# A two-layer hybrid decoder step: row sums on VectorE and the late states placed two to a step

## The chip, the cores and the metric

The kernel runs on one core of a Trainium2 chip. The number to be predicted is the device time of one execution in microseconds (us). In the text PE is TensorE, PEld its weight load, DVE is VectorE, ACT ScalarE, POOL GpSimd and SP SyncE.

## The reference

One inference step of a trunk with two layers, for a prompt of 512 tokens and 8 decode sequences of one token, 520 columns in all, in f32. Layer 0 mixes by a gated delta rule, layer 1 by a Mamba-2 scan; each layer goes on with a gated convolutional FFN, and each of the four residual sums is normalised:

```python
x = _layer_norm(DN_ALPHA * x + h, ln1_g[i], ln1_b[i])
f, fb = _conv_ffn(x, ffn_conv[i], ffn_w_up[i], ffn_conv_w[i], ffn_conv_b[i], ffn_w_down[i])
x = _layer_norm(DN_ALPHA * x + f, ln2_g[i], ln2_b[i])

def _conv_ffn(x, buf, w_up, conv_w, conv_b, w_down):
    gv = x @ w_up
    gate, val = gv[..., :D_FF], gv[..., D_FF:]
    gate, new_buf = _causal_dwconv(gate, buf, conv_w, conv_b)
    return (jax.nn.silu(gate) * val) @ w_down, new_buf
```

D_MODEL is 1024, D_FF 2816. Besides the rows, the step returns the new recurrent states of the 8 decode sequences. For layer 1 such a state is `h = exp(dt a) h + dt x B^T` for 32 heads of 64 x 128; these states are not needed by anything that follows in the step.

## The kernel before

Activations lie feature-major: 128 features by 520 columns, two halves h = 0 and 1 of 260. Products in f32 are made of three matmuls with f32r parts (high x high, low x high, high x low). A weight chunk (up to 8 blocks of 128 x 128, `prep`, L214) is loaded into one of two "raw" buffers by ScalarE's queue, its high part "hi" is cast by ScalarE (L229) and its low part "lo" subtracted by VectorE (L230), with three buffers of each; chunks are made two units ahead of TensorE. `unit` (L234) runs one output block: 24 matmuls a half in the up projection, 66 in the down projection, and then the evacuation of that half.

The plan is a list of units. Up projection: nine gate blocks for half 0, five for half 1, then steps m = 0 to 21 that each take gate block m + 4 (one half up to block 8, both from block 9 on) and value block m. A gate block's second half is convolved on VectorE (L423), and the evacuation of a value block makes f = s * psl on VectorE (L482, three buffers f), its high part fh on ScalarE and its low part fl on GpSimd (L285). Down projection: five blocks ("rows" 0 to 4) with both halves, then three blocks for half 0 and three for half 1, which is the tail. A scheduler orders the instructions of every engine before the run, and each engine keeps that order.

The last LayerNorm runs beside the down projection. `ln_evac` makes a row R (L335, or L332 and L312 in the tail) and adds it into the row sum lnacc (L341, L343, L345). After five rows "mean" is made on TensorE from lnacc, ScalarE copies it to lnshift (L347), and rows are shifted by it (L350) and squared (L367), the squares summed on GpSimd (L369). After the eighth row of a half `ln_half` makes "mean" and "var", and then rstd (L382 to L387), subtracts the mean (L390 on GpSimd, L392 on VectorE), multiplies by rstd (L397), scales (L399, L401) and stores o_y.

A late state is one half of the 8 sequences for one pair of heads of layer 1: 32 of them wait in the list `later`. `state` (L994) loads the old state Sd (256 KB) and a row Sr broadcast to 128 partitions (256 KB) by SyncE's queue, multiplies both (L1004, L1005), adds them (L1006), all on GpSimd, and stores o_sdec. A tiny copy of one column into each tile (L999, L1002) holds the load back until its step. `late` takes one state for each of the gate blocks m = 5 to 21 in the up projection, with two buffers of each tile, and three for each of rows 0 to 4 of the down projection, with one buffer. Layer 0 does the same with 16 states, all of which fit beside its up projection.

## Time and profile before

| what | us |
|---|---|
| runs shown | 1798.01, 1792.56, 1792.79 |
| median | 1792.79 |
| the profiled execution | 1798.44 |
| its span | 1796.6 |
| TensorE busy in the span | 1617.7 (90%) |
| VectorE busy | 1202.9 (67%) |
| ScalarE busy | 840.3 (47%) |
| GpSimd busy | 964.4 (54%) |

Busy shares are means over stages of different kind. The change lies in the last quarter: the second up projection ends at 1605.6 us of the span, where the second down projection begins. The first down projection begins at 717 us. Line numbers in the rows are those of the kernel before.

### The profile page before, as it was taken

Reading aid. Unit: us, or ns where it says so; the run is one execution under the profiler, and the core shown is the slowest. Engines: PE = TensorE matmul, PEld = TensorE weight load, DVE = VectorE, ACT = ScalarE, POOL = GpSimd, SP = SyncE. Lnnn points to the kernel's source line nnn. Section 1 sums busy time; section 2 is a strip of 40 time slices with the busy share of each in tenths; the row PEclk is TensorE's granted clock in tenths of the full one; section 3 lists DMA queues with packets and bytes.
Section 4 is the critical chain, followed back from the end, with each engine's and each line's share of the span. In section 5 each row is a group of like instructions: output and inputs, shape, how many; then the busy total and the mean of one; then the engine's idle time right before and its main releaser. Section 6 shows DMA issues by size and latency. Waiting matters only on the chain.

```text
span 1796.6 us, 33707 instructions
## 1 busy us (share of the span) xinstructions
PE 1617.7 (90%) x12889; PEld 1558.6 (87%) x12889; DVE 1202.9 (67%) x2133; ACT 840.3 (47%) x1724; POOL 964.4 (54%) x1090
## 2 busy tenths in 40 slices
PE   8888989898899999999978898989979999999683
PEld 7878888888799999998877797979978999999683
DVE  5967887767776554346799989876486774533255
ACT  4644664344564443125657455535246544432133
POOL 4844777554346554143355757575053565644656
PEclk9999998999999999999999899989999999999897
DMA  5422343234465443335554534332654655435454
GB/s 181 135 84 60 103 136 103 85 113 159 129 201 183 159 165 117 87 96 159 172 147 138 154 120 138 124 103 89 192 169 145 197 179 168 158 121 162 144 159 138
DMA packets 108978, 250.35 MB, mean 139 GB/s; under 512 B 15345, under 2 KB 31697, under 8 KB 108785
## 3 DMA queue, kind: packets, MB, share of 16 engines
q1 hardware_dynamic: 84048, 160.90, 28.3%
q10 hardware_dynamic: 24768, 87.30, 15.7%
q8 instruction: 101, 1.65, 0.4%
q14 instruction: 61, 0.49, 0.1%
HBM read 225.80 MB, written 22.92 MB: 138 GB/s over the span
## 4 chain that ended last, share of the span: by engine, by line
PE 44%; DVE 28%; DMA 13%; ACT 5%; POOL 5%; issue 4%; SPq 1%; ACTq 0%; DVEq 0%; POOLq 0%
PE psl L252 39%; DVE lo L230 4%; DVE sE L1198 3%; DVE y L423 2%; DMA raw<-w_down 2%; DMA Sd<-sstate 2%; ACT hi L229 2%; DMA raw<-w_up 1%; DVE Xtmp L828 1%; DVE kq L423 1%; DMA o_sdec<-Sd 1%; DVE sE L1202 1%; DVE dy L1256 1%; DMA gbc<-gd 1%; POOL Sd L1006 1%
## 5 line engine op out<-in xcount | busy, mean ns | idle before, releaser
L252 PE MATMUL psl<-XH,hi 128*128 128x260 f32 (+1 forms) x2816 | 816.2, 291 | 27.1 <-ACT u L603 8.7
L252 PE MATMUL psl<-XL,hi 128*128 128x260 f32 (+1 forms) x2848 | 822.9, 289 | 7.6 <-DVE XL L409 4.7
L252 PE MATMUL psl<-XH,lo 128*128 128x260 f32 (+1 forms) x2816 | 811.3, 289 | 6.6 <-DVE lo L230 6.2
L252 PEld LDWEIGHTS psl<-XH,hi 128*128 128x128 f32 (+1 forms) x2816 | 540.2, 192 | 36.8 <-ACT u L603 10.2
L230 DVE TENSOR_TENSOR lo<-raw,hi 128x512 fp32r<-128x512 f32 (+2 forms) x439 | 354.3, 842 | 304.6 <-ACT hi L229 300.2
L252 PEld LDWEIGHTS psl<-XL,hi 128*128 128x128 f32 (+1 forms) x2848 | 545.4, 192 | 13.9 <-DVE XL L409 6.2
L252 PEld LDWEIGHTS psl<-XH,lo 128*128 128x128 f32 (+1 forms) x2816 | 539.8, 192 | 13.7 <-DVE lo L230 9.5
L229 ACT CAST hi<-raw 128x512 fp32r<-128x512 f32 (+2 forms) x499 | 314.2, 669 | 401.5 <-PE psl L252 254.2
L252 PE MATMUL psl<-fh,lo 128*128 128x260 f32 x704 | 203.8, 290 | 3.5 <-DVE lo L230 3.4
L252 PE MATMUL psl<-fh,hi 128*128 128x260 f32 x704 | 203.5, 289 | 3.8 <-ACT hi L229 3.8
L252 PE MATMUL psl<-fl,hi 128*128 128x260 f32 x704 | 201.7, 287 | 0.0
L230 POOL TENSOR_TENSOR lo<-raw,hi 128x1024 fp32r<-128x1024 f32 x60 | 148.0, 2467 | 52.0 <-ACT hi L229 50.6
L252 PEld LDWEIGHTS psl<-fh,lo 128*128 128x128 f32 x704 | 135.5, 192 | 5.6 <-DVE lo L230 5.4
L252 PEld LDWEIGHTS psl<-fh,hi 128*128 128x128 f32 x704 | 135.6, 193 | 5.0 <-ACT hi L229 4.5
L252 PEld LDWEIGHTS psl<-fl,hi 128*128 128x128 f32 x704 | 135.3, 192 | 0.3
L285 POOL TENSOR_TENSOR fl<-f,fh 128x260 fp32r<-128x260 f32 x88 | 83.1, 944 | 38.2 <-ACT fh L284 38.2
L423 DVE SCALAR_TENSOR_TENSOR s<-u,par,s 128x512 f32<-128x512 f32 x88 | 77.9, 885 | 6.2 <-ACT s L420 4.4
L482 DVE TENSOR_TENSOR f<-s,psl 128x260 f32<-128x260 f32 x88 | 36.9, 420 | 60.6 <-PE psl L252 59.2
L1005 POOL TENSOR_TENSOR Sd<-Sd,ddt 128x512 f32<-128x512 f32 x32 | 37.0, 1156 | 73.4 <-DMA Sd<-sstate 73.4
L252 PE MATMUL psl<-y,hi 128*128 128x260 f32 x256 | 73.0, 287 | 1.0 <-POOL y L285 0.7
L284 ACT CAST fh<-f 128x260 fp32r<-128x260 f32 x88 | 35.8, 407 | 80.4 <-DVE f L482 80.4
L1006 POOL TENSOR_TENSOR Sd<-Sd,Sr 128x512 f32<-128x512 f32 x48 | 66.2, 1380 | 0.9
(399 smaller groups left out, 2676.2 us busy)
## 6 DMA issues: line engine op xcount, KB each, us to landing
raw<-w_up ACTq DMA_DIRECT2D x106, 512.0 KB
raw<-w_down ACTq DMA_DIRECT2D x44, 512.0 KB
raw<-w_sin SPq DMA_DIRECT2D x43, 512.0 KB
raw<-w_gin SPq DMA_DIRECT2D x32, 512.0 KB
Sd<-sstate SPq DMA_DIRECT2D x64, 256.0 KB
raw<-w_down ACTq DMA_DIRECT2D x22, 384.0 KB
Sd<-gstate SPq DMA_DIRECT2D x32, 256.0 KB
kb<-kr SPq DMA_DIRECT2D x32, 256.0 KB
```

The lines of the kernel that those rows point to most:

```text
L229: nc.scalar.copy(out=hi[:, ks, :mw], in_=raw[:, ks, :])
L230: eng.tensor_tensor(out=lo[:, ks, :mw], in0=raw[:, ks, :], in1=hi[:, ks, :mw].bitcast(F32), op=ALU.subtract)
L252: self.nc.tensor.matmul(out=ps[h][:mw], lhsT=w[:, b0 + k, :mw], rhs=x[:, hs], start=(k0 + k == first and i == 0), stop=(k0 + k == last and ...
L284: nc.scalar.copy(out=hi, in_=xf)
L285: (eng or nc.gpsimd).tensor_tensor(out=lo, in0=xf, in1=hi.bitcast(F32), op=ALU.subtract)
L423: nc.vector.scalar_tensor_tensor(out=y[:, :S], in0=u[:, j:j + S], scalar=self.pcol(wname, i * w + j), in1=y[:, :S], op0=ALU.mult, op1=ALU.add)
L482: nc.vector.tensor_tensor(out=f, in0=ss[m][:, hs], in1=ps, op=ALU.mult)
L828: nc.vector.tensor_tensor(out=tmp[:, :, :, i:], in0=_bc(X16[:, None, :, i:], [P, 2, C, n]), in1=D[:, i:i + 2, :, i:], op=ALU.mult)
L1005: nc.gpsimd.tensor_tensor(out=St, in0=St, in1=_bc(decay[:, :, None], D4), op=ALU.mult)
L1006: nc.gpsimd.tensor_tensor(out=St, in0=St, in1=t, op=ALU.add)
L1198: nc.vector.tensor_scalar(out=E[:, c, :], in0=E[:, c, :], scalar1=self.acum[:, c, h:h + 1], scalar2=0.0, op0=ALU.subtract, op1=ALU.min)
L1202: eng.tensor_tensor(out=E, in0=E, in1=CB, op=ALU.mult)
```

## The change

The row sums of the last LayerNorm (`lni == 3`) go to VectorE. `late` takes a count in place of a number of buffers: in the up projection two states at a gate block while more than 22 are left, else one, and two at each of rows 0 to 4 of the down projection. The tiles Sd and Sr have two buffers in both places. So 22 states lie beside the up projection (two at each of m = 5 to 9, one at each of m = 10 to 21), ten beside the down projection; before it was 17 and 15. Layer 0, with 16 states, keeps one at a gate block.

```diff
+        eng = nc.vector if self.lni == 3 else nc.gpsimd
         if n in (2, NS + 2):
-            nc.gpsimd.tensor_tensor(out=acc, in0=self.R[:, rows[-2], hs], in1=r, op=ALU.add)
+            eng.tensor_tensor(out=acc, in0=self.R[:, rows[-2], hs], in1=r, op=ALU.add)
         elif n not in (1, NS, NS + 1, KD):
-            nc.gpsimd.tensor_tensor(out=acc, in0=acc, in1=r, op=ALU.add)
+            eng.tensor_tensor(out=acc, in0=acc, in1=r, op=ALU.add)
         if n == NS:
-            nc.gpsimd.tensor_tensor(out=acc, in0=acc, in1=r, op=ALU.add)
+            eng.tensor_tensor(out=acc, in0=acc, in1=r, op=ALU.add)
...
-                                self.late(p, u[:, T:T + 1], 2)
+                                self.late(p, u[:, T:T + 1], 2 if len(self.later) > 22 else 1)
...
-                        self.late(lp, self.R[:, m, :1], 1)
+                        self.late(lp, self.R[:, m, :1], 2)
...
-    def late(self, p, after, bufs):
-
-        for _ in range(1 if bufs == 2 else 3):
+    def late(self, p, after, n):
+
+        for _ in range(n):
             if self.later:
                 f, *x = self.later.pop(0)
-                f(p, after, bufs, *x)
+                f(p, after, *x)
...
-        St = p.tile(D4, F32, tag="Sd", name="Sd", bufs=bufs)
+        St = p.tile(D4, F32, tag="Sd", name="Sd", bufs=2)
...
-        t = p.tile(D4, F32, tag="Sr", name="Sr", bufs=bufs)
+        t = p.tile(D4, F32, tag="Sr", name="Sr", bufs=2)
```

The scheduler's order of the two kernels is the same up to the second up projection on every engine. From there it differs on GpSimd and SyncE, from the second down row on VectorE, and from the fifth on ScalarE and TensorE. Lines of the changed kernel after L339 are one higher than those of before.

GpSimd in the second up projection, one step with its state, before:

```order
L999 COPY Sd_16555<-u_16544 128x1
L1002 COPY Sr_16558<-u_16544 128x1
L1005 TENSOR_TENSOR Sd_16555<-Sd_16555,ddt_10608 128x512
L285 TENSOR_TENSOR fl_15776<-f_16599,fh_15775 128x260
L451 MEMSET u_17195 128x2
L1004 TENSOR_TENSOR Sr_16558<-Sr_16558,xdd_10609 128x512
L285 TENSOR_TENSOR fl_15776<-f_16627,fh_15775 128x260
L1006 TENSOR_TENSOR Sd_16555<-Sd_16555,Sr_16558 128x512
L475 COPY cout_15781<-u_16664 128x10
```

The first step with two states, now, from the second state's copies on:

```order
L1000 COPY Sd_16445<-u_16424 128x1
L1003 COPY Sr_16448<-u_16424 128x1
L1006 TENSOR_TENSOR Sd_16435<-Sd_16435,ddt_10608 128x512
L1005 TENSOR_TENSOR Sr_16438<-Sr_16438,xdd_10609 128x512
L285 TENSOR_TENSOR fl_15776<-f_16489,fh_15775 128x260
L452 MEMSET u_17100 128x2
L1006 TENSOR_TENSOR Sd_16445<-Sd_16445,ddt_10608 128x512
L1007 TENSOR_TENSOR Sd_16435<-Sd_16435,Sr_16438 128x512
L1005 TENSOR_TENSOR Sr_16448<-Sr_16448,xdd_10609 128x512
L285 TENSOR_TENSOR fl_15776<-f_16517,fh_15775 128x260
L1007 TENSOR_TENSOR Sd_16445<-Sd_16445,Sr_16448 128x512
L476 COPY cout_15781<-u_16554 128x10
```

A step's two fl and the clearing of the next u stand between the parts of two states instead of one.

GpSimd about the fifth row of the second down projection, before (lnacc at L345 is the row sum that "mean" reads):

```order
L1005 TENSOR_TENSOR Sd_19574<-Sd_19574,ddt_10608 128x512
L1006 TENSOR_TENSOR Sd_19574<-Sd_19574,Sr_19577 128x512
L1002 COPY Sr_19587<-R_19026 128x1
L999 COPY Sd_19584<-R_19026 128x1
L345 TENSOR_TENSOR lnacc_19027<-lnacc_19027,R_19026 128x260
L312 TENSOR_TENSOR xr_20476<-XH_86,XL_87 128x260
L1004 TENSOR_TENSOR Sr_19587<-Sr_19587,xdd_10609 128x512
L345 TENSOR_TENSOR lnacc_19027<-lnacc_19027,R_19026 128x260
L312 TENSOR_TENSOR xr_20574<-XH_86,XL_87 128x260
L1005 TENSOR_TENSOR Sd_19584<-Sd_19584,ddt_10608 128x512
L350 TENSOR_TENSOR R_19026<-R_19026,lnshift_19028 128x260 x3
L1006 TENSOR_TENSOR Sd_19584<-Sd_19584,Sr_19587 128x512
```

The same place now, from the end of the state pair of row 3:

```order
L1007 TENSOR_TENSOR Sd_19790<-Sd_19790,Sr_19793 128x512
L312 TENSOR_TENSOR xr_20476<-XH_86,XL_87 128x260
L312 TENSOR_TENSOR xr_20574<-XH_86,XL_87 128x260
L351 TENSOR_TENSOR R_19076<-R_19076,lnshift_19078 128x260 x3
L370 TENSOR_TENSOR lnsq_19079<-lnsq_19079,sq_19972 128x260
L1000 COPY Sd_19987<-R_19076 128x1
L1003 COPY Sr_19990<-R_19076 128x1
L1000 COPY Sd_19997<-R_19076 128x1
L1003 COPY Sr_20000<-R_19076 128x1
L370 TENSOR_TENSOR lnsq_19079<-lnsq_19079,sq_19976 128x260
L351 TENSOR_TENSOR R_19076<-R_19076,lnshift_19078 128x260 x3
L370 TENSOR_TENSOR lnsq_19079<-lnsq_19079,sq_19980 128x260
```

The row sums are gone from here, and the shift by the mean stands ahead of the last pair of states. VectorE at the same place, before:

```order
L230 TENSOR_TENSOR lo_19929<-raw_19926,hi_19928 128x512 x2
L335 SCALAR_TENSOR_TENSOR R_19026<-xr_19952,psl_19812 128x260
L335 SCALAR_TENSOR_TENSOR R_19026<-xr_20025,psl_19813 128x260
L230 TENSOR_TENSOR lo_20054<-raw_20051,hi_20053 128x512
L230 TENSOR_TENSOR lo_20054<-raw_20051,hi_20053 128x256
L350 TENSOR_TENSOR R_19026<-R_19026,lnshift_19028 128x260
L332 SCALAR_TENSOR_TENSOR xr_20141<-xr_20141,lnshift_19028 128x260
```

And now:

```order
L230 TENSOR_TENSOR lo_19939<-raw_19936,hi_19938 128x512 x2
L335 SCALAR_TENSOR_TENSOR R_19076<-xr_19962,psl_19822 128x260
L346 TENSOR_TENSOR lnacc_19077<-lnacc_19077,R_19076 128x260
L335 SCALAR_TENSOR_TENSOR R_19076<-xr_20025,psl_19823 128x260
L346 TENSOR_TENSOR lnacc_19077<-lnacc_19077,R_19076 128x260
L230 TENSOR_TENSOR lo_20054<-raw_20051,hi_20053 128x512
L230 TENSOR_TENSOR lo_20054<-raw_20051,hi_20053 128x256
L351 TENSOR_TENSOR R_19076<-R_19076,lnshift_19078 128x260 x2
```

Each row sum stands right behind the row that it takes in. On TensorE the first "mean" stands behind 671 of the 1056 down matmuls, before behind 674; in the first down projection it stands behind 674 in both.

GpSimd's last instructions, before:

```order
L1002 COPY Sr_19990<-R_19026 128x1
L999 COPY Sd_19987<-R_19026 128x1
L1004 TENSOR_TENSOR Sr_19990<-Sr_19990,xdd_10609 128x512
L1005 TENSOR_TENSOR Sd_19987<-Sd_19987,ddt_10608 128x512
L1006 TENSOR_TENSOR Sd_19987<-Sd_19987,Sr_19990 128x512
L1002 COPY Sr_20000<-R_19026 128x1
L999 COPY Sd_19997<-R_19026 128x1
L390 TENSOR_TENSOR R_19026<-R_19026,pc_20352 128x260
L1004 TENSOR_TENSOR Sr_20000<-Sr_20000,xdd_10609 128x512
L1005 TENSOR_TENSOR Sd_19997<-Sd_19997,ddt_10608 128x512
L390 TENSOR_TENSOR R_19026<-R_19026,pc_20671 128x260 x5
L1006 TENSOR_TENSOR Sd_19997<-Sd_19997,Sr_20000 128x512
```

And now:

```order
L1007 TENSOR_TENSOR Sd_19987<-Sd_19987,Sr_19990 128x512
L370 TENSOR_TENSOR lnsq_19079<-lnsq_19079,sq_20039 128x260
L1007 TENSOR_TENSOR Sd_19997<-Sd_19997,Sr_20000 128x512
L370 TENSOR_TENSOR lnsq_19079<-lnsq_19079,sq_20043 128x260
L370 TENSOR_TENSOR lnsq_19079<-lnsq_19079,sq_20047 128x260
L370 TENSOR_TENSOR lnsq_19079<-lnsq_19079,sq_20145 128x260
L370 TENSOR_TENSOR lnsq_19079<-lnsq_19079,sq_20244 128x260
L391 TENSOR_TENSOR R_19076<-R_19076,pc_20352 128x260 x5
L370 TENSOR_TENSOR lnsq_19079<-lnsq_19079,sq_20480 128x260
L370 TENSOR_TENSOR lnsq_19079<-lnsq_19079,sq_20579 128x260
L391 TENSOR_TENSOR R_19076<-R_19076,pc_20671 128x260 x5
```

No state stands between or behind the subtractions of the two halves (pc is the mean, copied). On VectorE the eight products of the first half (L398 now) stand ahead of the tail's last three evacuations; before, seven of them stood ahead of the last one and the eighth behind it.

## Rows read from the trace of the kernel before

**Rows 1.** Busy time of each engine in seven stretches, the first three of the first down projection, the last four of the second; columns are the stretch, its length, busy us and instructions of PE, PEld, DVE, ACT and POOL, the granted TensorE clock, the busy share of the DMA engines and GB/s.

```profile
717.00:797.70 80.70, 80.70 (x677) 80.70 (x676) 26.50 (x43) 17.30 (x33) 15.16 (x18) 1.00 0.31 90
797.70:823.30 25.60, 24.07 (x193) 23.48 (x192) 18.95 (x26) 12.37 (x28) 17.64 (x20) 1.00 0.43 122
823.30:855.00 31.70, 28.54 (x210) 27.29 (x209) 22.16 (x44) 19.10 (x42) 8.15 (x8) 0.95 0.54 163
1605.70:1686.40 80.70, 80.70 (x675) 80.55 (x673) 26.79 (x41) 16.37 (x31) 37.62 (x48) 1.00 0.48 149
1686.40:1701.50 15.10, 0.06 (x1) 0.00 (x0) 1.96 (x2) 0.92 (x2) 7.42 (x11) 0.59 0.48 154
1701.50:1733.00 31.50, 27.62 (x189) 26.74 (x190) 19.60 (x24) 9.48 (x20) 21.65 (x23) 0.87 0.42 134
1733.00:1767.00 34.00, 28.68 (x209) 27.17 (x207) 20.42 (x28) 14.44 (x31) 23.59 (x26) 0.95 0.52 161
```

**Rows 2.** The down projection's matmuls on TensorE with the low part of f, in the first and in the second layer: count, shortest, median and longest ns, first and last start.

```profile
L252 PE MATMUL psl<-fl,hi x352: 276/283/421, 717.1 to 854.7; 128*128 128x260 f32 x176
...
L252 PE MATMUL psl<-fl,hi x352: 276/283/473, 1605.7 to 1766.5; 128*128 128x260 f32 x176
```

**Rows 3.** Waits of all engines, of 797 to 860 us (the first row, the tail of the first down projection) and of 1686 to 1797 us (the others): total us, times, longest.

```profile
ACT hi L229 <- DMA raw<-w_down: 10.6, 9, 2.3
...
ACT hi L229 <- DMA raw<-w_down: 24.5, 9, 7.6
...
PE mean L360 <- POOL lnacc L345: 15.1, 1, 15.1
```

**Rows 4.** GpSimd's time line beside the fifth row of the second down projection: start, us, what, and in brackets the idle time before it and what ended it.

```profile
1691.33 0.18 POOL L999 COPY Sd<-R 128x1 f32<-128x1 f32 x1 [1.87 <-DMA o_sdec<-Sd]
1693.45 1.04 POOL L1004 TENSOR_TENSOR Sr<-Sr,xdd 128x512 f32<-128x512 f32 x1 [1.94 <-DMA Sr<-bd]
1696.15 1.05 POOL L1005 TENSOR_TENSOR Sd<-Sd,ddt 128x512 f32<-128x512 f32 x1 [1.67 <-DMA Sd<-sstate]
1697.28 1.26 POOL L1006 TENSOR_TENSOR Sd<-Sd,Sr 128x512 f32<-128x512 f32 x1
...
1700.63 0.18 POOL L999 COPY Sd<-R 128x1 f32<-128x1 f32 x1 [1.84 <-DMA o_sdec<-Sd]
1700.77 0.73 POOL L345 TENSOR_TENSOR lnacc<-lnacc,R 128x260 f32<-128x260 f32 x1
1701.45 0.73 POOL L312 TENSOR_TENSOR xr<-XH,XL 128x260 f32<-128x260 f32 x1
```

**Rows 5.** TensorE's "var" matmuls with the last square of a half, in the first down projection (first row) and the second: count, ns, first and last start.

```profile
L360 PE MATMUL var<-sq,mean x4: 382/510/641, 829.5 to 858.7; 128*128 128x260 f32 x4
...
L360 PE MATMUL var<-sq,mean x4: 383/512/641, 1760.2 to 1773.5; 128*128 128x260 f32 x4
```

**Rows 6.** The time line of the end: GpSimd, then ScalarE, then VectorE.

```profile
1776.47 1.05 POOL L1005 TENSOR_TENSOR Sd<-Sd,ddt 128x512 f32<-128x512 f32 x1 [0.39 <-DMA Sd<-sstate]
...
1781.54 0.73 POOL L390 TENSOR_TENSOR R<-R,pc 128x260 f32<-128x260 f32 x1
1783.16 1.04 POOL L1004 TENSOR_TENSOR Sr<-Sr,xdd 128x512 f32<-128x512 f32 x1 [0.89 <-DMA Sr<-bd]
...
1785.21 3.86 POOL L390 TENSOR_TENSOR R<-R,pc 128x260 f32<-128x260 f32 x5
...
1782.83 0.39 ACT L382 ACTIVATE rstd<-mean 128x260 f32<-128x260 f32 x1 [10.36 <-DVE R L397]
1783.11 0.37 ACT L384 COPY pc<-mean 128x260 f32<-128x260 f32 x1
...
1782.31 0.43 DVE L397 TENSOR_TENSOR R<-R,rstd 128x260 f32<-128x260 f32 x1 [10.34 <-POOL R L390]
```

**Rows 7.** GpSimd's time line in the second up projection, one step of the plan.

```profile
1417.04 0.71 POOL L999 COPY Sd<-u 128x1 f32<-128x1 f32 x1
...
1421.53 1.05 POOL L1005 TENSOR_TENSOR Sd<-Sd,ddt 128x512 f32<-128x512 f32 x1 [3.67 <-DMA Sd<-sstate]
1422.54 1.22 POOL L285 TENSOR_TENSOR fl<-f,fh 128x260 fp32r<-128x260 f32 x1
...
1423.76 1.45 POOL L1004 TENSOR_TENSOR Sr<-Sr,xdd 128x512 f32<-128x512 f32 x1
1425.17 1.20 POOL L285 TENSOR_TENSOR fl<-f,fh 128x260 fp32r<-128x260 f32 x1
1426.33 1.29 POOL L1006 TENSOR_TENSOR Sd<-Sd,Sr 128x512 f32<-128x512 f32 x1
1427.55 0.68 POOL L475 COPY cout<-u 128x10 f32<-128x10 f32 x1
```

**Rows 8.** VectorE's time line in the same stage: the low parts of one weight chunk, and the convolution L423 twice.

```profile
1414.54 2.50 DVE L230 TENSOR_TENSOR lo<-raw,hi 128x512 fp32r<-128x512 f32 x2 [1.11 <-ACT hi L229]
...
1418.04 0.74 DVE L423 SCALAR_TENSOR_TENSOR s<-u,par,s 128x512 f32<-128x512 f32 x1
...
1426.65 1.52 DVE L423 SCALAR_TENSOR_TENSOR s<-u,par,s 128x512 f32<-128x512 f32 x1
```

**Rows 9.** Busy time of each engine in 20 us of the same stage, columns as in rows 1.

```profile
1420.00:1440.00 20.00, 20.00 (x170) 20.00 (x169) 15.84 (x20) 10.06 (x21) 13.84 (x18) 1.00 0.59 188
```

**Rows 10.** TensorE's groups of 600 to 900 us: the "mean" matmuls with the row sum, count, busy us, mean ns, and idle time ahead of them.

```profile
L360 PE MATMUL mean<-lnacc,mean 128*128 128x260 f32 x8 | 2.4, 381 | 0.0
```

More of the change, by code (lines that the diff above doesn't have):

```diff
@@ L987, in gdn_decode, with gdn_state, state @@
             self.later.append((self.gdn_state, h, i, kr))
-    def gdn_state(self, p, after, bufs, h, i, kr):
+    def gdn_state(self, p, after, h, i, kr):
         bs = slice(i * B // 2, (i + 1) * B // 2)
-        self.state(p, after, bufs, self.a["gstate"][:, h, bs], kr[0, bs], self.deg[:, h, bs], self.vn[:, h, bs], self.a["o_gdec"][:, h, bs])
-    def state(self, p, after, bufs, src, row, decay, col, dst):
+        self.state(p, after, self.a["gstate"][:, h, bs], kr[0, bs], self.deg[:, h, bs], self.vn[:, h, bs], self.a["o_gdec"][:, h, bs])
+    def state(self, p, after, src, row, decay, col, dst):
         nc = self.nc
         D4 = [P, B // 2, P]
-        St = p.tile(D4, F32, tag="Sd", name="Sd", bufs=bufs)
+        St = p.tile(D4, F32, tag="Sd", name="Sd", bufs=2)
         nc.gpsimd.tensor_copy(out=St[:, 0, :1], in_=after)
         nc.sync.dma_start(out=St, in_=src)
-        t = p.tile(D4, F32, tag="Sr", name="Sr", bufs=bufs)
+        t = p.tile(D4, F32, tag="Sr", name="Sr", bufs=2)
         nc.gpsimd.tensor_copy(out=t[:, 0, :1], in_=after)
@@ L1261, in ssd_decode, with ssd_state @@
         nc.vector.scalar_tensor_tensor(out=x[:, S:], in0=x[:, S:], scalar=self.pcol("sd", i), in1=y, op0=ALU.mult, op1=ALU.add)
-    def ssd_state(self, p, after, bufs, i, j, bd):
+    def ssd_state(self, p, after, i, j, bd):
         bs = slice(j * B // 2, (j + 1) * B // 2)
-        self.state(p, after, bufs, self.a["sstate"][:, i, bs], bd[0][bs], self.ddt[:, bs, 1, i], self.xdd[:, i, bs], self.a["o_sdec"][:, i, bs])
+        self.state(p, after, self.a["sstate"][:, i, bs], bd[0][bs], self.ddt[:, bs, 1, i], self.xdd[:, i, bs], self.a["o_sdec"][:, i, bs])
     def ssd_norm(self, p, g):
```

## The prediction

> **What bounds the kernel now.** I read the stretches first. Beside rows 0 to 4 of the second down projection (1605.7 to 1686.4) TensorE is busy all of 80.70 us at a granted clock of 1.00 (2.4 GHz); then come 15.10 us with 0.06 us of work, and two stretches at 27.62 of 31.50 and 28.68 of 34.00 us [rows 1]. The same projection of layer 0 has no late states beside it and runs the same 1056 matmuls with the LayerNorm's in nearly the same places. Its first 80.70 us are equal to the microsecond; it has no hole, and the rest takes 25.60 + 31.70 us [rows 1]. From first to last matmul the one takes 137.6 us, the other 160.8 [rows 2]. This twin is my main measure.
>
> The waits say who made the hole: "mean" on TensorE waited 15.1 us for GpSimd's last row sum, L345 [rows 3]. The time line of GpSimd shows why that was late. The sum is two-fifths of a microsecond's worth of VectorE work and 0.73 us on GpSimd, but it stands behind a state whose two loads and one store go in turn through one buffer: 1.87 us for the store, 1.94 and 1.67 for the loads, 3.35 us of arithmetic (1.04 + 1.05 + 1.26) [rows 4]. A state takes 9.30 us (1691.33 to 1700.63), and GpSimd takes its instructions in order.
>
> The end has the same cause once more. TensorE's last instruction starts at 1773.5 [rows 5] and ends some 0.4 us later, but the square that follows on ScalarE starts at 1782.83, after 10.36 us for VectorE's L397, which itself waited 10.34 us for one subtraction of GpSimd (L390 at 1781.54). That one stood behind the state whose L1005 ran at 1776.47 [rows 6].
>
> **The change part by part.** The profiled execution took 1798.44 us, its span 1796.6; the median of the three shown is 1792.79, from 1792.56 to 1798.01. I sum the change in the span, and take it off the median.
>
> *Row sums on VectorE.* Twelve adds leave GpSimd, 12 x 0.73 = 8.8 us [rows 4], and come to VectorE at the 0.43 us of its add of this shape [rows 6], 5.2 us; ten of them lie beside rows 0 to 4, where VectorE worked 26.79 of 80.70 us [rows 1] and casts are made ahead. The sum now follows the add that makes the row, and the order puts "mean" on TensorE behind 671 down matmuls, not 674. TensorE comes there with the whole of row 4 done, so the sum of the first half is long there. The hole closes: 15.1 us, less at most one evacuation and one add (0.9 us) if the first half's sum is held behind the second's. The part that waits newly is VectorE: nothing but the subtractions for the next weights is queued behind it, and those chunks lie ahead of TensorE.
>
> *No states in the tail.* Ten states instead of fifteen, two to a row, two buffers. A row lasts 80.70 / 5 = 16.1 us; two states need 2 x 3.35 us of GpSimd, four tiny copies (0.7) and two xr (1.5) [rows 4], 8.9 us, and some 4 us of loading before the first (3.67 in [rows 7]). This fits, so states 1 to 8 are done with their rows; the last pair stands behind the mean's subtractions and comes in the tail, 7.4 us of GpSimd among the squares' sums, where the twin's GpSimd worked 17.64 of 25.60 us [rows 1]. After that no state is left. The tail took 31.5 + 34.0 = 65.5 us, the twin's 57.3; ScalarE waited 24.5 us for w_down here and 10.6 there [rows 3]. A gain of 0 (the weights' own chain stays as it is) to 8.2 (the twin); I take 6, near the twin, less 2 us for the last pair, since its traffic and arithmetic are all that is left of the cause. From the last down matmul (1766.5) to the last "var" (1773.5) it took 7.0 us, in the twin 858.7 - 854.7 = 4.0 [rows 2, 5], since here VectorE's last evacuation stood behind the first half's products; in the new order, as in the twin's, they come before the last three evacuations. 0 to 3.0, I take 3.0.
>
> *The end.* With no state ahead, the five subtractions of the first half stand in one piece and are long done. The step from 1773.9 to 1782.83 goes: 8.9 us. What is late next is the second half's own chain: square, reciprocal, root, products. There GpSimd's five subtractions (3.86 us) began at 1785.21, behind the last state, whose L1004 ran at 1783.16, while their operand was there at about 1783.5 [rows 6]: 0 to 1.7 us, I take 1.7, since the products of VectorE end right behind them. The last o_sdec store goes too, which I leave at nothing: the o_y stores end the program and lie behind it only in part.
>
> *Five states more beside the up projection.* This is the cost. In the five steps from m = 5 two states run where one ran. GpSimd's cycle of 1417.04 to 1428.17 holds 0.71 + 0.18 + 1.05 + 1.22 + 1.45 + 1.20 + 1.29 + 0.68 = 7.8 us and one wait of 3.67 us for a load [rows 7]. A second state adds 1.05 + 1.45 + 1.29 and its copies, 4.1 us: 11.9 us, and 15.6 if the wait stays. TensorE takes 72 matmuls a step up to m = 8 and 96 after: at 80.70 us for 677 [rows 1], 0.119 each, that is 8.6 and 11.4 us. So GpSimd falls behind in four steps and comes up again in the twelve with one state. Its fl may be late by a step and a half (three f buffers); what is nearer is VectorE, whose L423 takes 1.52 us beside GpSimd's work and 0.74 without [rows 8], and which makes the weights' low parts. TensorE was at 20.00 of 20.00 us there [rows 9], but not by much: the chunk whose low parts ended at 1414.54 + 2.50 = 1417.0 [rows 8] is that of val 3, with 1560 up matmuls from its first to the end of the stage (its own 48, gate 8's 24, 31 units of 48), so 186 us before 1605.6, at 1419.6. The margin is 2.6 us. VectorE loses at most half of GpSimd's added 4.1 us, and it is busy about seven tenths of the time (15.84 of 20.00 [rows 9]): 1.5 us a step, 6 in four, less the margin: 3 us on the path. Least 0 (the lag stays within the buffers); most 13: five states of 3.35 and their copies, 18.5 us, wholly on the path, less the margin and the 2.8 us that the fifth step is longer. I take 3, since the lag was there before ([rows 7]: no gap but the load's) and never reached TensorE. SyncE's queue holds only states there, and u's reloads are issued before them.
>
> SBUF's port speaks against this part. The two L423 rows differ by a factor of two with the neighbour's work [rows 8]. The Trainium skill, "SBUF — State Buffer", section "Who interferes with whom", says that VectorE and GpSimd share a port pair as an exclusive lock, so that one blocks for the other's whole instruction. By that rule the added states would be the 13 us of the upper end and not 3. The trace agrees in direction; whether the pair is as exclusive as that, no row here separates.
>
> *Sum*: 15.1 + 6 + 3.0 + 8.9 + 1.7 - 3 = 31.7 us. The span would be 1764.9, the profiled time about 1767, and from the median 1792.79 - 31.7 = 1761.1. **I predict 1761 us.**
>
> **The rivals.** *The up projection pays* (0.18). For it: the factor of two [rows 8] and the margin of 2.6 us. Against: GpSimd's own gap of 3.67 us a step [rows 7] in which VectorE runs alone. 13 us in place of 3: 1771.
>
> *The tail is the weights' own* (0.15). For it: ScalarE waited for w_down in the twin too [rows 3], and the last pair of states still runs there. Then 0 for the tail and for its last evacuation: 9 us less, 1770.
>
> *The hole moves to VectorE* (0.06): it evacuates in order, behind subtractions that wait for casts, and "mean" waits for its sum. Against: in the twin "mean" had no idle time ahead of it [rows 10], though GpSimd's sum waited for the same evacuation and then took longer. Half of the hole left and the tail's gain gone: 31.7 - 7.5 - 9 = 15 us, 1778. That the states don't lie where the change says is excluded by the order, which has 22 of them on GpSimd ahead of the down rows.
>
> *Slower* (0.03): the doubled steps are paced by GpSimd with both loads unhidden, each 4.1 + 3.7 = 7.8 us longer, 39 us in five, less the margin 36; the gains of 34.7 are gone, and a hole's lower clock after it (0.87 over 31.5 us [rows 1], 4.1 us) makes 1799. It decides from 40 us of TensorE idle beside the up projection, 8 a step. Against: two buffers let the second load run under the first state's arithmetic.
>
> **How the numbers follow.** My forecast has 0.58, with 1752 to 1766: all terms at their good ends give 15.1 + 8.2 + 3.0 + 8.9 + 1.7 = 36.9, so 1756, and the runs differ by 5.5 us among themselves, of which I allow 4 below and 5 above. The range goes to the first two rivals with the same allowance, 1752 to 1777, and leaves out the last two and the corner in which the first two come together (1780). About 0.3% is what a measurement of this kernel tells from no change, 5.4 us. Faster by more than that are the forecast and three rivals but for a rest: 0.94; the same 0.03 (a hole wholly moved, or 30 us paid beside the up projection); slower 0.03.
>
> **What would show it.** Right: no wait of "mean" above 1 us; first to last down matmul 138 to 144 us; no state on GpSimd after the second mean but one pair; the last "var" to the end in 12 to 13 us; the first down matmul at 1606 to 1611. Wrong in the up term: TensorE under 20 us of 20 between 1405 and 1460, waiting for lo or hi. Wrong in the tail: ScalarE again over 20 us behind w_down. The prediction falls if the first down matmul comes after 1620, or if "mean" waits for L346.

## The result, and the profile after

The changed kernel takes 1762.92 us (median of 1763.92, 1761.31, 1769.49 and 1761.92) against 1792.67 of the kernel before (four runs, 1789.72 to 1798.01): 0.9838 of the time, 95% interval 0.9803 to 0.9872. The forecast was 1761. That the sum came so near is in part luck: the gains were larger than forecast, the cost of the up projection was more than twice as large, and the largest term came out for a reason other than the one given.

To see where the time went I cut each profiled span at four events that every variant here has. They are the copy of a gate block's first half into u, early in the second up projection; the first matmul with fl of the second down projection; the last such matmul; and the last "var". The next fence has the three rows for the changed kernel: one of ScalarE's time line, and TensorE's matmuls with fl and its "var" as in [rows 2] and [rows 5].

```profile
1358.13 0.37 ACT L433 COPY u<-psl 128x260 f32<-128x260 f32 x1
...
L252 PE MATMUL psl<-fl,hi x352: 277/283/420, 1609.9 to 1748.9; 128*128 128x260 f32 x176
...
L361 PE MATMUL var<-sq,mean x4: 382/418/487, 1724.8 to 1750.6; 128*128 128x260 f32 x4
```

So the pieces are 1609.9 - 1358.13 = 251.8 ("up"), 1748.9 - 1609.9 = 139.0 ("down"), 1.7 ("var"), and 1762.1 - 1750.6 = 11.5 to the end of the span ("end"). The same for all kernels of this study, from one profile each, in us; "start" is the time of the copy, before which all of them run the same program (but that e6 and e11 have six buffers of f in layer 0 too):

| kernel | start | up | down | var | end | span |
|---|---|---|---|---|---|---|
| before | 1361.5 | 244.2 | 160.8 | 7.0 | 23.1 | 1796.6 |
| changed | 1358.1 | 251.8 | 139.0 | 1.7 | 11.5 | 1762.1 |
| e1_row_sums | 1354.9 | 244.5 | 159.0 | 5.1 | 15.4 | 1778.9 |
| e2_states | 1359.7 | 251.8 | 138.6 | 1.8 | 11.5 | 1763.4 |
| e3_17_15 | 1355.9 | 244.1 | 156.3 | 1.7 | 11.5 | 1769.5 |
| e4_none_up | 1358.5 | 244.6 | 137.9 | 1.8 | 11.6 | 1754.4 |
| e5_none_down | 1359.6 | 250.5 | 137.6 | 1.7 | 11.6 | 1761.0 |
| e6_f6 | 1358.9 | 244.3 | 137.0 | 1.8 | 11.5 | 1753.5 |
| e8c_load_ahead | 1354.2 | 245.1 | 137.2 | 1.8 | 11.5 | 1749.7 |
| e9_one_buffer | 1357.3 | 251.4 | 153.7 | 1.7 | 11.5 | 1775.6 |
| e10_17_15_shift | 1355.5 | 244.2 | 153.5 | 1.7 | 11.5 | 1766.4 |
| e11_f6_24_8 | 1356.0 | 247.5 | 136.3 | 1.8 | 11.5 | 1753.1 |

"Start" differs by up to 7.3 us from run to run, so a span is compared by its pieces. From before to after the change gives 21.8 (down) + 5.3 (var) + 11.6 (end) and takes 7.6 (up): 31.1 us, where the sum was 31.7.

The down projection has no hole any more. Busy time by stretches, columns as in [rows 1], from the first down matmul with fl to the last, the first stretches as long as those there:

```profile
1609.90:1690.60 80.70, 80.70 (x660) 80.70 (x660) 36.12 (x50) 18.03 (x35) 43.89 (x53) 0.97 0.57 175
1690.60:1705.70 15.10, 15.10 (x123) 14.82 (x121) 13.75 (x19) 7.17 (x17) 13.49 (x17) 1.00 0.54 162
1705.70:1737.20 31.50, 27.51 (x208) 25.77 (x206) 24.98 (x38) 16.19 (x33) 17.63 (x17) 1.00 0.58 178
1737.20:1749.40 12.20, 11.42 (x86) 10.59 (x86) 5.50 (x12) 4.46 (x10) 1.75 (x2) 1.00 0.44 142
```

In the waits, what answers to [rows 3] is 16.7 us of ScalarE behind w_down instead of 24.5, and no wait at all of the "mean" of the fifth row instead of 15.1. The half microsecond that is left belongs to the last "mean", which waits at 1749.80 for the last evacuation:

```profile
ACT hi L229 <- DMA raw<-w_down: 16.7, 9, 3.6
...
PE mean L361 <- DVE R L312: 0.5, 1, 0.5
```

At the fifth row GpSimd (time line, answer to [rows 4]) is through with row 3's pair at 1687.7. It waits for VectorE, and shifts the rows as soon as ScalarE has the mean; the last pair of states runs behind that:

```profile
1686.39 1.28 POOL L1007 TENSOR_TENSOR Sd<-Sd,Sr 128x512 f32<-128x512 f32 x1
1689.33 0.99 POOL L312 TENSOR_TENSOR xr<-XH,XL 128x260 f32<-128x260 f32 x1 [1.65 <-DVE R L335]
1691.47 0.98 POOL L312 TENSOR_TENSOR xr<-XH,XL 128x260 f32<-128x260 f32 x1 [1.15 <-DVE R L335]
1693.18 2.53 POOL L351 TENSOR_TENSOR R<-R,lnshift 128x260 f32<-128x260 f32 x3 [0.73 <-ACT lnshift L348]
```

At the end (answer to [rows 6]) the five subtractions wait for the mean and for nothing else, and the products of VectorE follow:

```profile
1750.83 0.37 ACT L385 COPY pc<-mean 128x260 f32<-128x260 f32 x1
...
1751.28 3.49 POOL L391 TENSOR_TENSOR R<-R,pc 128x260 f32<-128x260 f32 x5 [9.60 <-ACT pc L385]
...
1754.73 2.81 DVE L398 TENSOR_TENSOR R<-R,rstd 128x260 f32<-128x260 f32 x8 [0.49 <-ACT rstd L388]
```

What the up projection pays shows in these rows: the window that answers to [rows 9], TensorE's instructions that waited longest (the last of them at the end of the stage), what VectorE did ahead of the first of them, and the waits of the whole stage:

```profile
1420.00:1440.00 20.00, 19.03 (x159) 18.82 (x159) 15.34 (x19) 9.97 (x20) 13.93 (x19) 1.00 0.65 211
...
1431.79 0.39 PE L252 MATMUL psl<-XH,lo 128*128 128x260 f32 x1 [0.97 <-DVE lo L230]
1581.41 0.39 PE L252 MATMUL psl<-XH,lo 128*128 128x260 f32 x1 [0.46 <-DVE lo L230]
1593.85 0.39 PE L252 MATMUL psl<-XH,lo 128*128 128x260 f32 x1 [0.63 <-DVE lo L230]
1609.55 0.56 PE L252 MATMUL psl<-fh,hi 128*128 128x260 f32 x1 [4.12 <-DVE f L483]
...
1429.93 2.96 DVE L230 TENSOR_TENSOR lo<-raw,hi 128x512 fp32r<-128x512 f32 x2 [0.94 <-ACT hi L229]
...
POOL Sd L1006 <- DMA Sd<-sstate: 60.6, 17, 6.2
DVE f L483 <- POOL fl L285: 36.4, 10, 5.4
DVE f L483 <- POOL u L452: 20.7, 6, 6.1
```

These are 0.97 + 0.46 + 0.63 + 4.12 = 6.2 of the 7.6 us; the rest I have not placed. The matmuls right behind the last wait ran slower, and nearly all of that falls into the piece "down". In the first 5 us of that piece the changed kernel has 27 matmuls at a granted clock of 0.57, between the two levels of 1.2 and 2.4 GHz. The variant e6_f6 below, in which TensorE does not stand there, has 44 at 1.00 (the second row):

```profile
1609.90:1614.90 5.00, 5.00 (x27) 5.00 (x27) 3.75 (x6) 2.90 (x7) 3.39 (x4) 0.57 0.65 185
...
1603.20:1608.20 5.00, 5.00 (x44) 5.00 (x43) 1.45 (x3) 1.19 (x3) 1.27 (x2) 1.00 0.36 108
```

The 17 matmuls that are missing take 2.0 us at 0.119 us each. So by an estimate from these rows the up projection pays some 9.6 us in all, and at full clock "down" would be 137.0 us, as it is in e6_f6.

### The profile page after: what moved, and what is told of

Its sections match the earlier page's. It is cut to its first block, busy times and chain, and to the rows that moved or that the text cites. A ratio compares the mean times of both kernels' runs of the same rounds, so it can differ in the third digit from the quotient of the medians.

```text
span 1762.1 us, 33677 instructions
## 1 busy us (share of the span) xinstructions
PE 1608.4 (91%) x12889; PEld 1549.9 (88%) x12889; DVE 1210.0 (69%) x2143; ACT 836.8 (47%) x1724; POOL 958.7 (54%) x1080
## 4 chain that ended last, share of the span: by engine, by line
PE 36%; DVE 28%; DMA 16%; POOL 8%; ACT 6%; issue 5%; SPq 1%; ACTq 0%; DVEq 0%; POOLq 0%
PE psl L252 31%; DVE lo L230 4%; DMA Sd<-sstate 3%; DMA raw<-w_down 3%; DVE sE L1199 2%; DMA raw<-w_up 2%; ACT hi L229 2%; DVE y L424 2%; POOL Sd L1007 1%; DMA Sr<-bd 1%; POOL fl L285 1%; DVE Xtmp L829 1%; DVE kq L424 1%; POOL Sr L1005 1%; DVE dy L1257 1%
## 5 line engine op out<-in xcount | busy, mean ns | idle before, releaser
L252 PEld LDWEIGHTS psl<-XH,lo 128*128 128x128 f32 (+1 forms) x2816 | 538.2, 191 | 15.4 <-DVE lo L230 11.1
L230 DVE TENSOR_TENSOR lo<-raw,hi 128x512 fp32r<-128x512 f32 (+2 forms) x439 | 359.8, 854 | 255.3 <-ACT hi L229 249.9
L424 DVE SCALAR_TENSOR_TENSOR s<-u,par,s 128x512 f32<-128x512 f32 x88 | 81.3, 923 | 6.9 <-ACT s L421 5.1
L1006 POOL TENSOR_TENSOR Sd<-Sd,ddt 128x512 f32<-128x512 f32 x32 | 37.3, 1167 | 67.5 <-DMA Sd<-sstate 67.4
L1007 POOL TENSOR_TENSOR Sd<-Sd,Sr 128x512 f32<-128x512 f32 x48 | 70.3, 1465 | 0.3
```

The source lines that it names most:

```text
L230: eng.tensor_tensor(out=lo[:, ks, :mw], in0=raw[:, ks, :], in1=hi[:, ks, :mw].bitcast(F32), op=ALU.subtract)
L252: self.nc.tensor.matmul(out=ps[h][:mw], lhsT=w[:, b0 + k, :mw], rhs=x[:, hs], start=(k0 + k == first and i == 0), stop=(k0 + k == last and ...
L424: nc.vector.scalar_tensor_tensor(out=y[:, :S], in0=u[:, j:j + S], scalar=self.pcol(wname, i * w + j), in1=y[:, :S], op0=ALU.mult, op1=ALU.add)
L1006: nc.gpsimd.tensor_tensor(out=St, in0=St, in1=_bc(decay[:, :, None], D4), op=ALU.mult)
L1007: nc.gpsimd.tensor_tensor(out=St, in0=St, in1=t, op=ALU.add)
```

## The experiments

Median times stand against 1797.71, 1796.85 and 1796.82 us of the kernel before, run beside the variants of the same group. In brackets behind a median stand the lowest and the highest run, behind a ratio its 95% interval.

**One part at a time.** The first variant is the kernel before with the row sums on VectorE alone.

```diff
+        eng = nc.vector if self.lni == 3 else nc.gpsimd
...
-            nc.gpsimd.tensor_tensor(out=acc, in0=acc, in1=r, op=ALU.add)
+            eng.tensor_tensor(out=acc, in0=acc, in1=r, op=ALU.add)
```

> The kernel before with the last norm's row sums on VectorE and nothing else; 17 and 15 states, one buffer beside the down projection. By my sum: the wait of mean (15.1 us) goes, tail and end stay, so about 1778 us, first to last down matmul about 146, from the last var to the end still some 22 us. Rival 'the chain of states paces the end': fifteen states of 9.3 us on GpSimd stay as they were, the subtractions for the outputs still stand among them, and only the twelve adds of 0.73 us leave GpSimd, so the hole closes but the end comes at most 9 us sooner: 1784 us or more, with the step before the last output over 25 us. Rival 'row sums are all': 1765 or less.

Measured: 1784.03 us, 0.9918 (0.9895 to 0.9941). "Mean" no longer waits for a row sum, but the down projection is only 1.8 us shorter. The time of the first rival is met, its reason not quite: the end took 15.4 us, 7.7 less than before, which would fit the 8.8 us of adds that left GpSimd; and the hole did not close. It came back at another place. TensorE's first wait of the tail, ScalarE's time line and GpSimd's:

```profile
1705.90 0.58 PE L252 MATMUL psl<-fh,hi 128*128 128x260 f32 x1 [13.92 <-ACT hi L229]
...
1703.96 0.42 ACT L368 ACTIVATE lnsq<-R 128x260 f32<-128x260 f32 x1 [15.14 <-POOL R L351]
...
1705.24 1.12 ACT L229 CAST hi<-raw 128x512 fp32r<-128x512 f32 x2
...
1701.98 1.26 POOL L1007 TENSOR_TENSOR Sd<-Sd,Sr 128x512 f32<-128x512 f32 x1
1703.20 2.11 POOL L351 TENSOR_TENSOR R<-R,lnshift 128x260 f32<-128x260 f32 x3
```

The mean is there, but the shift by it (L351) stands on GpSimd behind the states. ScalarE's square waits 15.14 us for the shift, and the cast for the next weights is queued behind the square: TensorE waits 13.92 us for "hi" in place of 15.1 for "mean".

The second variant is the changed kernel with the sums left on GpSimd:

```diff
-        eng = nc.vector if self.lni == 3 else nc.gpsimd
+        eng = nc.gpsimd
```

> The changed kernel with the row sums back on GpSimd; 22 and ten states, two buffers. My theory: with two buffers and two states a row GpSimd is done with row 3's pair before row 4 is evacuated, so the last sum is late by an add and an xr at most: mean waits 0 to 2 us, 1762 to 1765 us. Rival 'the row sums close the hole': mean waits some 10 us for the last sum on GpSimd again, 1772 us or more.

Measured: 1764.52 us (1762.11 to 1765.21), 0.9808 (0.9788 to 0.9828); "mean" waits for no sum, down 138.6 us. The row sums are neither enough to close the hole nor needed for it.

**The split.** One state at each gate block and three at each row, with the rest of the change:

```diff
-                                self.late(p, u[:, T:T + 1], 2 if len(self.later) > 22 else 1)
+                                self.late(p, u[:, T:T + 1], 1)
...
-                        self.late(lp, self.R[:, m, :1], 2)
+                        self.late(lp, self.R[:, m, :1], 3)
```

> The changed kernel with one state at each gate block and three at each down row, so 17 and 15 as before, but two buffers and the row sums on VectorE. My theory: the second up projection is back at its old length (7.5 us shorter than in the changed kernel), mean does not wait, and the end is free as long as the last three states are done before the subtractions: 3 x 3.35 = 10 us of GpSimd in the tail in place of 7, so 1757 to 1762 us. Rival 'the number of states in the tail decides': the tail and the end get long again, 1768 us or more, and the move of five states was the point of the change.

Measured: 1771.91 us, 0.9856 (0.982 to 0.9892). The up projection and the end came as I expected, the down projection did not: 156.3 us. The rival's number is met; the time lies at the fifth row again, though, by the same chain as in e1 (TensorE, ScalarE, GpSimd):

```profile
1699.13 0.58 PE L252 MATMUL psl<-fh,hi 128*128 128x260 f32 x1 [9.56 <-ACT hi L229]
...
1698.15 0.42 ACT L368 ACTIVATE lnsq<-R 128x260 f32<-128x260 f32 x1 [9.67 <-POOL R L351]
...
1694.79 1.26 POOL L1007 TENSOR_TENSOR Sd<-Sd,Sr 128x512 f32<-128x512 f32 x1
1696.01 1.42 POOL L312 TENSOR_TENSOR xr<-XH,XL 128x260 f32<-128x260 f32 x2
1697.39 2.12 POOL L351 TENSOR_TENSOR R<-R,lnshift 128x260 f32<-128x260 f32 x3
```

The buffers alone:

```diff
+        nb = 2 if self.stage == "up" else 1
-        St = p.tile(D4, F32, tag="Sd", name="Sd", bufs=2)
+        St = p.tile(D4, F32, tag="Sd", name="Sd", bufs=nb)
...
-        t = p.tile(D4, F32, tag="Sr", name="Sr", bufs=2)
+        t = p.tile(D4, F32, tag="Sr", name="Sr", bufs=nb)
```

> The changed kernel with one buffer of Sd and Sr beside the down projection (two a row, ten states, row sums on VectorE). My theory after the runs so far: what matters is whether GpSimd is through with its states when the fifth row is done. With one buffer a state takes 9.3 us, two 18.6 against 16.1 of a row, so GpSimd is some 10 us behind, and its shift by the mean holds ScalarE's square and the cast queued behind it: one wait of TensorE for hi of 6 to 14 us, first to last down matmul 146 to 154, 1768 to 1777 us. Rival 'ten states are few enough, the second buffer does nothing': 1761 to 1765 us.

Measured: 1777.36 us, 0.9894 (0.988 to 0.9909), the upper edge of my range; down 153.7 us, one wait of TensorE of 9.02 us for "hi", and ScalarE's square 9.73 us behind L351:

```profile
1706.89 0.58 PE L252 MATMUL psl<-fh,hi 128*128 128x260 f32 x1 [9.02 <-ACT hi L229]
...
1705.91 0.42 ACT L368 ACTIVATE lnsq<-R 128x260 f32<-128x260 f32 x1 [9.73 <-POOL R L351]
```

So two states a row and two buffers are both needed: with either one alone "down" is 14.7 or 17.3 us longer than in the changed kernel.

To test the chain itself I took the shifts and the sums of squares off GpSimd in the variant with 17 and 15:

```diff
-                (nc.vector if i % 2 else nc.gpsimd).tensor_tensor(out=d, in0=d, in1=shift, op=ALU.subtract)
+                (nc.vector if i % 2 or self.lni == 3 else nc.gpsimd).tensor_tensor(out=d, in0=d, in1=shift, op=ALU.subtract)
...
-            nc.gpsimd.tensor_tensor(out=acc, in0=acc, in1=sq, op=ALU.add)
+            eng = nc.vector if self.lni == 3 else nc.gpsimd
+            eng.tensor_tensor(out=acc, in0=acc, in1=sq, op=ALU.add)
```

> The variant with 17 and 15 states (three a row, two buffers, row sums on VectorE), and the last norm's shifts by the mean and sums of squares made by VectorE as well, so that ScalarE's squares no longer hang on GpSimd. My theory: there TensorE waited 9.6 us for hi, whose cast stood on ScalarE behind a square that waited for GpSimd's shift behind the states; that wait goes, first to last down matmul falls from 156.3 to 147 or less, 1758 to 1764 us. Rival 'the cast was late for its load': the wait of some 9 us stays, 1770 us. Rival 'the xr of the tail rows, still on GpSimd behind the states, hold VectorE instead': a wait for lo or hi of 5 us or more, 1766 us or more.

Measured: 1771.31 us, 0.9862 (0.9844 to 0.9879), as without the edit. The third of the expectations came true: the wait of 9.56 us went, and the tail rows' xr, left on GpSimd behind the states, made a new one. Taking the xr off GpSimd as well was not tried. GpSimd, VectorE, ScalarE and TensorE in turn:

```profile
1709.78 0.73 POOL L312 TENSOR_TENSOR xr<-XH,XL 128x260 f32<-128x260 f32 x1
...
1710.55 1.47 DVE L332 SCALAR_TENSOR_TENSOR xr<-xr,lnshift 128x260 f32<-128x260 f32 x1 [7.57 <-POOL xr L312]
...
1712.39 0.42 ACT L368 ACTIVATE sq<-R 128x260 f32<-128x260 f32 x1 [7.97 <-DVE lnsq L371]
1712.72 1.12 ACT L229 CAST hi<-raw 128x512 fp32r<-128x512 f32 x2
...
1713.37 0.59 PE L252 MATMUL psl<-fh,hi 128*128 128x260 f32 x1 [6.63 <-ACT hi L229]
```

**What the states cost.** Without those beside the up projection, and without those beside the down projection:

```diff
-                                self.late(p, u[:, T:T + 1], 2 if len(self.later) > 22 else 1)
+                                n = 2 if len(self.later) > 22 else 1
+                                if l:
+                                    del self.later[:n]
+                                else:
+                                    self.late(p, u[:, T:T + 1], n)
```

> The changed kernel without the 22 states beside the second up projection (22 of the 32 o_sdec blocks are not written). My theory: the 22 states cost 7.5 us there and the 17 of before cost nothing, so from the first matmul of the first down projection to that of the second it takes 888 to 889 us, as in the kernel before, against 896.3 in the changed one; about 1754 us. Rival 'the states always cost there': below 884, and 1750 or less. Rival 'the up projection was not longer at all, the profiled runs differ': 895 to 897.

Measured: 1756.18 us, one run; up 244.6 us. From the first down matmul of layer 0 (713.4) to that of layer 1 (1603.1) it is 889.7, 0.7 above what I had named; by the nearer event, the copy, it is as long as with 17 states (244.1 to 244.5). So 17 states cost nothing there and 22 cost 7.2 to 7.6 us.

```diff
-                        self.late(lp, self.R[:, m, :1], 2)
+                        del self.later[:2]
```

> The changed kernel without the ten states beside the second down projection (10 of the 32 o_sdec blocks are not written). My theory: the ten states there cost next to nothing any more: first to last down matmul 136.7 to 138 (139.0 with them, 136.7 in layer 0), from the last var to the end 11 us as with them, so 1759 to 1762 us. Rival 'the last pair of states still costs in the tail': 134 us or less from first to last, 1757 or less.

Measured: 1762.82 us, one run, 0.8 above my range; down 137.6 us. The ten states cost 1.4 us there at most: half a microsecond of it (4 matmuls of 0.119 us) is the lower clock at the start of the piece, where this run has 31 matmuls in the first 5 us and the changed kernel 27. Four kernels with ten states (e2, e4, e6, e8c) lie between 137.0 and 138.6.

**Why five more states cost 7.6 us.** Six buffers for f:

```diff
-                        f = p.tile([P, HT], F32, tag="f", name="f", bufs=3)
+                        f = p.tile([P, HT], F32, tag="f", name="f", bufs=6)
```

> The changed kernel with six buffers for f in place of three. Measure of the up projection: from the copy of gate 7's first half into u (ScalarE, 1358.13 in the changed kernel) to the first down matmul with fl; that is 251.8 us in the changed kernel, 244.2 in the one before, 244.6 without states. My theory: GpSimd's queue sets the pace through f (VectorE stood 43 us for GpSimd there), so with three more buffers VectorE and TensorE run on: 244.2 to 246.5, and about 1756 to 1760 us in all, the lag being hidden behind the first down row, which needs the last fl only at its end. Rival 'VectorE is slowed at the memory by GpSimd's added work': f's buffers change nothing, 250 us or more.

Measured: 1754.17 us (1751.99 to 1757.28), 0.9761 (0.9735 to 0.9786); up 244.3. That is below my range, since "down" fell by 2.0 us as well. GpSimd is still late, but it now hurts nobody. Its time line at the end of the stage has seven fl in a row, and VectorE's last f waits for TensorE and not for GpSimd:

```profile
1597.60 5.89 POOL L285 TENSOR_TENSOR fl<-f,fh 128x260 fp32r<-128x260 f32 x7
...
1603.33 0.42 DVE L483 TENSOR_TENSOR f<-s,psl 128x260 f32<-128x260 f32 x1 [2.43 <-PE psl L252]
```

Loads one step ahead, the main lines of the edit:

```diff
+        ready, self.loaded = self.loaded, []
...
+        for f in ready:
+            f(after)
...
+        nb = 4 if self.ahead else 2
...
+        def compute(nxt=None):
+            c, d = col, decay
+            if nxt is not None:
+                cg = p.tile([P, 2, B // 2], F32, tag="cg", name="cg", bufs=4)
+                nc.gpsimd.tensor_copy(out=cg[:, :, :1], in_=_bc(nxt[:, :, None], [P, 2, 1]))
+                nc.gpsimd.tensor_copy(out=cg[:, 0], in_=col)
+                nc.gpsimd.tensor_copy(out=cg[:, 1], in_=decay)
+                c, d = cg[:, 0], cg[:, 1]
...
+            self.loaded.append(compute)
```

> The changed kernel, but beside the second up projection a state's two loads are issued one step ahead of its arithmetic (four buffers of Sd and Sr there, and three tiny copies more for each state on GpSimd); the last step's state is computed after the stage. My theory: GpSimd no longer waits some 5 us a step for a load, a step with one state takes it 7 us of TensorE's 11.4, so the lag of the doubled steps is made up: 244.2 to 247 us by the same measure. Rival 'arithmetic and memory, not the load waits': 250 us or more. Rival 'the copies into the next buffers wait for the store before': some 3 us less than in the changed kernel, 248 to 249.

Measured: 1753.14 us (1751.47 to 1754.13), 0.9755 (0.9736 to 0.9773); up 245.1. A step with one state now ends with GpSimd waiting for the plan (ScalarE's copy into u) and no longer for a load:

```profile
1514.78 0.52 POOL L476 COPY cout<-u 128x10 f32<-128x10 f32 x1 [3.01 <-ACT u L447]
...
1526.24 0.52 POOL L476 COPY cout<-u 128x10 f32<-128x10 f32 x1 [4.11 <-ACT u L447]
```

In the changed kernel GpSimd's steps go like this (the first product of a state at four steps, and the fl left at the end):

```profile
1485.19 1.53 POOL L1006 TENSOR_TENSOR Sd<-Sd,ddt 128x512 f32<-128x512 f32 x1 [1.29 <-DMA Sd<-sstate]
...
1529.34 1.05 POOL L1006 TENSOR_TENSOR Sd<-Sd,ddt 128x512 f32<-128x512 f32 x1 [4.95 <-DMA Sd<-sstate]
...
1578.35 1.05 POOL L1006 TENSOR_TENSOR Sd<-Sd,ddt 128x512 f32<-128x512 f32 x1 [4.67 <-DMA Sd<-sstate]
...
1590.80 1.05 POOL L1006 TENSOR_TENSOR Sd<-Sd,ddt 128x512 f32<-128x512 f32 x1 [4.80 <-DMA Sd<-sstate]
...
1605.97 3.69 POOL L285 TENSOR_TENSOR fl<-f,fh 128x260 fp32r<-128x260 f32 x4
```

TensorE takes 11.4 us a step. From 1485.19 to 1529.34 lie four steps of 11.0 us each, in which GpSimd makes up a little. From 1529.34 to 1590.80 lie five of 12.3 us, the last of 12.45 with 4.80 of it waiting; one load kept GpSimd waiting for 6.16 us, and from 1554 on an xr of 0.74 us comes to each step. Over the nine steps it is 11.7 us: GpSimd does not catch up. In e6 the same nine steps took 10.6 us each, and GpSimd waited 3.2 to 4.6 us for a load instead of 4.7 to 6.2; so e6 did more than hide the lag, and why the loads came sooner is not shown.

VectorE's slowness is not the cause: its convolution (L424, L423 in the kernel before; from 1400 to 1590 us) took 748 ns a piece without states and 941 in the changed kernel, but 993 in the kernel before and 969 and 994 in these two variants, and in those three "up" was within 0.5 us of that without states.

Last, more states to the up projection with six buffers:

```diff
-                                self.late(p, u[:, T:T + 1], 2 if len(self.later) > 22 else 1)
+                                self.late(p, u[:, T:T + 1], 2 if len(self.later) > 18 else 1)
...
-                        f = p.tile([P, HT], F32, tag="f", name="f", bufs=3)
+                        f = p.tile([P, HT], F32, tag="f", name="f", bufs=6)
```

> The changed kernel with six buffers of f and 24 states beside the up projection (doubled at seven gate blocks), eight beside the down projection (none at the fifth row). My theory: with six buffers the up projection stays at 244.3 to 246 us by the measure above, and the last pair of states, which cost 1.4 us at most, leaves the tail: 1752 to 1755 us, the same as with 22 and ten. Rival 'more states than 22 use up f's buffers': 247 us or more there, 1757 us or more.

Measured: 1755.85 us (1754.82 to 1756.87), 0.9778 (0.9762 to 0.9794). Up 247.5, so by the pieces two more states cost 3.2 us, and gave back 0.7 in the down projection; the rival's size there, though the total stayed a microsecond below its 1757. The rival's reason is not shown: TensorE waited 1.33 us for "lo" between 1420 and 1440 and never for f; the rest I have not placed. The intervals of this ratio and of that with 22 states and six buffers overlap. No split that was tried is better than 22 and ten with six buffers of f or with the loads ahead; the intervals of those two overlap.

## Why the prediction was right, point by point

- **The hole, 15.1 us.** Its size and its end were right; its owner was not. The step *Row sums on VectorE* said that the hole closes because the adds leave GpSimd. e1 closes the wait of "mean" and keeps 13.92 us of it as a wait for "hi"; e2 closes it without moving an add. What closes it is that GpSimd is through with its states when the fifth row is done (e2, e3, e9). The forecast held because the change did both, and that is luck. I had followed the wait to the last instruction (L345) and to the state ahead of it [rows 4], but priced only the first of three things on GpSimd that TensorE needs there: the sum, the shift and the xr.
- **The tail, 6 of 0 to 8.2.** Hole and tail gave 21.8 together, forecast 21.1. With the 2.0 us of lower clock that the up projection left at the start of the piece they gave 23.8, a little above the good end of both (23.3). "What is left of the cause" was the last pair, taken at 2 us; all ten states cost 1.4 at most (e5). That ScalarE's wait for w_down came from the states, as I took it, is not shown. Without any state beside the down projection (e5) 14.5 of its 24.5 us stay, and in e3, with fifteen states, it is 9.2:

```profile
ACT hi L229 <- DMA raw<-w_down: 14.5, 9, 2.3
```

- **Last down matmul to last var, 3.0 at most.** It gave 5.3. The bound was the twin's 4.0; 1.7 or 1.8 came out here and in every variant but e1. The trace of the kernel before shows why the twin was no bound: layer 1 follows it. The twin's last square starts on ScalarE at 857.68, behind a cast that waited 2.80 us for weights of the next layer, and TensorE runs 24 matmuls of that layer first (ScalarE, then TensorE):

```profile
856.73 1.05 ACT L229 CAST hi<-raw 128x1024 fp32r<-128x1024 f32 x1 [2.80 <-DMA raw<-w_sin]
...
858.50 0.60 PE L360 MATMUL var<-sq,mean 128*128 128x260 f32 x2
```

- **The end, 8.9 + 1.7.** It gave 11.6, so 11.5 us were left, below the 12 to 13 named. With no state among the subtractions it is 11.5 or 11.6 us in the changed kernel and nine variants; in e1, where L1006 still stands among them, 15.4.
- **The up projection, 3 of 0 to 13: mis-sized, 7.6, and some 9.6 with the lower clock behind it.** The step that failed is that GpSimd "comes up again in the twelve with one state". No cycle was set against TensorE's 11.4 us for it; the 7.8 us of work alone would allow it. But [rows 7] shows a cycle of 11.13 us with the wait in it, and in-order GpSimd has to stand through it: a margin of 0.3 us a step. Over nine such steps of the changed kernel the cycle was 11.7 us, with waits of 4.7 to 6.2, and the margin was gone. So the lag reached the end of the stage, where four fl were still to be made, and f's three buffers carried it to VectorE and TensorE. By itself either remedy takes it away: a longer queue (e6), or the wait taken out of the cycle (e8c). The sign that was named against this term came true: TensorE at 19.03 of 20 us between 1420 and 1440, waiting for "lo".
- **SBUF's port.** By the rule of the Trainium skill, "SBUF — State Buffer", section "Who interferes with whom", I had named 13 us as the price of the up projection. VectorE is slowed, as the traces show: L424, with two operands in SBUF, takes 748 ns without states and 941 in the changed kernel, and f, with one operand in PSUM, 424 and 419 ns. The same section says that an instruction with at most one SBUF input, outside the 2-port modes, does not contend, and the trace agrees. But of the waits that are placed the slowing can own no more than one, of a microsecond. The wait of 0.97 us at 1431.79 stands behind two pieces of lo that took 2.96 us, and VectorE had waited for nothing of GpSimd till then. The other three waits follow those of f, for which VectorE stood 57 us waiting for GpSimd in the changed kernel and 1.4 in the one before.
- **The rivals.** "The up projection pays" was right in direction, and half in size by the piece. "The tail is the weights' own" would have left 145.7 us from first to last down matmul, and it is 139.0. "Slower" asked for 40 us of TensorE idle beside the up projection, and the four longest waits make 6.2; its sum comes to 1798, not 1799. "The hole moves" names what e1 and e3 show, on ScalarE rather than VectorE; in the changed kernel nothing of it was left.

## What to carry to other kernels

When one in-order engine holds up another, list everything on it that the waiting engine will need next, not only the instruction that the wait names: here the sum, the shift and the xr took turns, and moving one or two off the engine bought little in that stage (1.8 us in e1, 2.8 in e10) while the states stayed ahead of them. Whether an engine can make up a lag is read from its whole cycle with its waits in it, against the cycle of the engine it serves; its busy time alone does not tell. A short queue between two engines (three buffers of f) turns a lag that would harm nobody into a stall, and three more buffers can be the cheapest cure.

## What the runs showed that I had not expected

- The same instructions up to the second up projection took 1354.2 to 1361.5 us in twelve profiles, 7.3 us of spread, more than several terms of this study. Pieces between events of one trace agreed better: "up" with 17 states or none within 0.5 us (244.1 to 244.6), with 22 states and three buffers of f within 1.3 (250.5 to 251.8).
- One wait of 4.12 us of TensorE was followed by a granted clock of 0.57 over the next 5 us, in which 27 matmuls started where 44 do at 1.00. By the estimate above the wait cost about half as much again as its own length.
- VectorE's subtraction for "lo" took 688 ns without states, 989 in the changed kernel and 1147 with the loads ahead, and this last kernel has the lowest median of all (its interval overlaps that of e6).
